# A two-layer hybrid block: the Fourier branch folded about the middle, three kinds of products as plain float32, steps reordered

## The chip, the cores and the metric

The kernel runs on one core of a Trainium2 chip. The metric is device time in microseconds (us) of one execution; lower is better. Engines are named PE or TensorE (matrix products; PEld is its weight load), DVE or VectorE, ACT or ScalarE, POOL or GpSimd, and SP or SyncE, whose queue issues nearly all transfers from HBM.

## The reference, cut to what matters

A backbone block of two layers over 512 latent tokens and 256 context tokens, 1024 channels, all float32. Each layer has a token-mixing part and a SwiGLU part. The mixing part projects the normed and modulated tokens (one matrix, 1792 columns) into three groups:

- A, 512 channels: a depthwise convolution, then an RG-LRU in both directions. Its gates are `sigmoid(xh @ wa + ba)` and `sigmoid(xh @ wx + bx)` with 64 x 64 blocks per head and direction.
- B, 256 channels: spatial gating. In chunks of 128 positions, `s = ws[h] @ v + bs`, with v normed, then `u * s`.
- C, 256 channels in four heads of 64: the Fourier branch, below.

```python
def fourier_mix(xf, wf):
    Bsz, L, _ = xf.shape
    z = xf.reshape(Bsz, L, H_C, HEAD_DIM).astype(jnp.float32)
    f = jnp.fft.fft2(z, axes=(1, 3), norm="ortho").real
    return jnp.einsum("blhc,hce->blhe", f, wf.astype(jnp.float32)).reshape(Bsz, L, D_C).astype(xf.dtype)
```

The three group outputs are RMS-normed, joined and projected by `w_out`. In the second layer the context is only read: its gates and scans are computed, the rest of its mixing is not.

## The kernel before

Tokens lie in six tiles of 128 positions: two of context, four of latents; the second layer's mixing handles the four latent tiles and runs only the RG-LRU over all six. The tokens are kept transposed (`XT`, channel by token), as a high and a low float32r part. `mm` forms a product from three float32r products, high x high, high x low, low x high (`self.pe.matmul`, all recorded on line 134). So every operand needs two parts: `split` copies the rounded value (ScalarE, line 208) and subtracts it from the source (line 203; VectorE or GpSimd, by `wsub` for weights). `split_psum` does the same out of PSUM (lines 873 to 878). A float32 operand can also be given to `matmul` as it is, which the kernel does for the modulation blocks (`mod_part`), the position rows at the start, sums over channels and diagonals.

`mixing` runs one letter of `STEPS[l]` after the other. The letters that matter: `a` the last of four projections with convolution (the first three come from the stage before); `e` the four gates of one 128-channel block of group A (`lru_gates`); `p` the activations of a block's scans, `s` one direction of its scan (`lru_scans`); `Z`, `V`, `U` take weights, `z` projects one half of the Fourier channels, `v` and `u` two tiles of the gating's halves; `f`, `w` small maps of the Fourier and gating branches; `c` the Fourier products over channels; `g` one gate projection of group A's output; `m` one modulation block; `R` rows of the gate after the output projection; `t` the spatial products; `L` releases all gelus, which until then are held so that ScalarE's tables need not change; a digit sets how much of the SBUF arena the loads leave free; `D` moves the weights' subtracts to VectorE.

While `pe.fixed` is true TensorE keeps exactly this written order; each other engine has an in-order queue whose order the framework chose when it built the program. Behind the steps, in the old kernel, come the transposes of group B (`put_group`), the sums of squares of group A, and `fourier`: per tile of positions, products with full cosine and sine matrices (12 products of 256 columns for a context tile, 24 for a latent tile), an RMS norm of that tile (`rms`: ScalarE square, GpSimd power, VectorE scale), transposes and a split. Group A's scaling (`group_a`) stands between the context and the latent tiles. Then `pe.fixed` ends and the output projection follows; its products, as soon as their operands stand, may slip ahead into gaps.

Weights are 512 KB units in a written list (`plan`), loaded ahead on SP's queue as the arena has room, and split when used or up to two units earlier. The output weights (`out`) are scaled and split by ScalarE (line 1353) and VectorE (line 1354). `psum_aux` has two buffers, `psum_big` three.

Of the kernel before, what the change touches and what calls it, by code (L numbers as in the profile page):

```python
# [45 lines left out]
BETWEEN = 2  # L46
# [114 lines left out]
class Kernel:  # L161
# [133 lines left out]
    def consts(self):  # L295
# [21 lines left out]
        self.spl = cp.tile([P, 2, 8], F32, tag="spl", name="spl")  # L317

# [461 lines left out]
    def conv_split(self, cv):  # L780
        xh, xl = self.buf(TOK), self.buf(TOK)
        self.split(xh.r, xl.r, cv[0].f)
        cv += [xh, xl]

    def lru_gates(self, l, m, cv):
        nc, par = self.nc, self.par
        u = self.gw[m // 2]
        if len(cv) == 1:
            self.conv_split(cv)
        xc, xh, xl = cv  # L790
# [14 lines left out]
        xh.free()  # L805
        xl.free()
# [73 lines left out]
    def fourier_maps(self, l):  # L880
# [3 lines left out]
        bd = [self.buf(512), self.buf(512)]  # L884
# [4 lines left out]
        self.split_psum(bd[0].r, bd[1].r, ps)  # L889
# [3 lines left out]
    def gating_maps(self, l):  # L893
        u = self.use(f"sg{l}")
        ws = [self.buf(512), self.buf(512)]
# [3 lines left out]
        self.split_psum(ws[0].r, ws[1].r, ps)  # L899
# [3 lines left out]
    def fourier_in(self, u, lo):  # L903
# [19 lines left out]
    def fourier(self, l, tiles, zc, between):  # L923
# [615 lines left out]
```

## Time and profile before

| | |
|---|---|
| median of 3 runs | 1506.51 us (1502.71 to 1507.05) |
| the profiled execution | 1506.1 us, its span 1504.1 us |
| TensorE busy | 1416.7 us, 94% of the span |
| VectorE busy | 893.4 us |
| ScalarE busy | 551.7 us |
| GpSimd busy | 294.8 us |
| mean granted TensorE clock | 0.974 of 2.4 GHz |
| read from HBM | 160.25 MB |

The span reaches from the first to the last instruction; the execution's own time lies 2.0 us above it. A busy TensorE is not one at its peak: matrix products are pipelined, and their recorded lengths overlap. A granted clock of 1.00 is 2.4 GHz, 0.50 is 1.2 GHz; a mean between them is a mixture of the two over time.

### The profile page before, as it was taken

The numbers are of one execution on the slowest core, as the hardware profiler recorded it, in microseconds if no ns is written. First come the engines' busy times: TensorE is split into PE (matmuls) and PEld (weight loads), VectorE is DVE, ScalarE is ACT, GpSimd is POOL, SyncE is SP. The second block draws the span as 40 slices with busy tenths as digits, with TensorE's granted clock in tenths as the row PEclk, the third lists the DMA queues.
The fourth block names the chain that finished last, engine by engine and source line by source line (L and its number), as shares of the span: only waits on it lengthen the run. The fifth ranks groups of instructions, "written<-read, shape, count | busy, mean of one in ns | idle before, by whom it ended". The sixth has DMA issues, their size and how long they took to land.

```text
span 1504.1 us, 18734 instructions
## 1 busy us (share of the span) xinstructions
PE 1416.7 (94%) x7527; PEld 1197.2 (80%) x7527; DVE 893.4 (59%) x1259; ACT 551.7 (37%) x784; POOL 294.8 (20%) x190
## 2 busy tenths in 40 slices
PE   6999888999999999999999998959998999999997
PEld 3788756779888888888888878858777888888885
DVE  6749756779527439443527396688788343353427
ACT  4576445345312202111203146886536232322210
POOL 3303323230021030030030044223230111020201
PEclk9999999999999999999999999969999999999999
DMA  9503365317116216244127004015427352242201
GB/s 329 139 15 99 105 224 186 97 31 236 43 43 211 70 55 198 71 139 162 36 77 231 28 29 128 1 48 169 127 67 228 98 154 71 70 130 60 77 14 56
DMA packets 169430, 163.56 MB, mean 109 GB/s; under 512 B 10456, under 2 KB 126648, under 8 KB 169344
## 3 DMA queue, kind: packets, MB, share of 16 engines
q1 hardware_dynamic: 169232, 162.08, 34.4%
q8 instruction: 59, 0.97, 0.3%
q0 software_dynamic: 112, 0.30, 0.1%
q14 instruction: 27, 0.22, 0.0%
HBM read 160.25 MB, written 2.10 MB: 108 GB/s over the span
## 4 chain that ended last, share of the span: by engine, by line
PE 72%; DVE 12%; ACT 5%; issue 3%; DMA 3%; POOL 3%; SPq 2%; DVEq 0%; POOLq 0%; ACTq 0%
PE mm L134 67%; PE aux L134 5%; POOL smalls L232 2%; DVE f L678 1%; DVE f L203 1%; DVE f L1220 1%; DMA f<-in_w_in_dram 1%; DVE r L203 1%; SPq L1315 1%; POOL r L203 1%; SPq L1333 1%; DVE f L832 1%; DVE smalls L709 1%; ACT r L208 1%; DVE f L835 1%
## 5 line engine op out<-in xcount | busy, mean ns | idle before, releaser
L134 PE MATMUL mm<-r,r 128*128 128x512 f32 (+1 forms) x6192 | 1230.6, 360 | 21.0 <-DVE f L1220 7.3
L134 PEld LDWEIGHTS mm<-r,r 128*128 128x128 f32 x6192 | 1035.7, 191 | 202.0 <-DVE f L1220 12.5
L208 ACT ACTIVATE r<-f 128x1024 fp32r<-128x1024 f32 (+2 forms) x244 | 227.1, 951 | 578.0 <-PE mm L134 267.9
L203 DVE TENSOR_TENSOR r<-f,r 128x1024 fp32r<-128x1024 f32 (+3 forms) x245 | 266.8, 1111 | 133.8 <-ACT r L208 119.9
L203 POOL TENSOR_TENSOR f<-f,f 128x1024 f32<-128x1024 f32 (+2 forms) x44 | 109.7, 2493 | 654.3 <-DVE f L1220 479.3
L1220 DVE TENSOR_TENSOR f<-mm,f 128x512 f32<-128x512 f32 (+1 forms) x80 | 76.2, 952 | 145.2 <-PE mm L134 145.1
L203 POOL TENSOR_TENSOR r<-f,r 128x1024 fp32r<-128x1024 f32 (+2 forms) x59 | 107.0, 1823 | 226.0 <-ACT r L208 159.3
L1235 DVE TENSOR_TENSOR f<-mm,f 128x768 f32<-128x768 f32 (+1 forms) x44 | 36.2, 823 | 176.0 <-PE mm L134 176.0
L134 PE MATMUL aux<-r,r 128*128 128x256 f32 (+1 forms) x780 | 112.5, 306 | 25.3 <-DVE r L878 10.7
L134 PEld LDWEIGHTS aux<-r,r 128*128 128x128 f32 x780 | 106.5, 211 | 32.5 <-DVE r L878 12.7
L232 POOL TENSOR_TENSOR smalls<-smalls,neghalf 128x1 f32<-128x1 f32 (+2 forms) x69 | 67.2, 975 | 255.1 <-DVE smalls L231 245.7
L573 DVE SCALAR_TENSOR_TENSOR f<-f,stc,f 128x512 f32<-128x512 f32 x140 | 102.3, 762 | 2.8 <-DMA f<-in_w_mod_dram 1.3
L203 DVE TENSOR_TENSOR f<-f,f 128x512 f32<-128x512 f32 (+1 forms) x66 | 61.7, 939 | 9.8 <-ACT f L801 8.1
L1234 ACT ACTIVATE f<-mm 128x768 f32<-128x768 f32 (+1 forms) x44 | 30.7, 699 | 95.7 <-PE mm L134 95.7
L134 PE MATMUL aux<-cst,f 128*128 128x128 f32 (+2 forms) x259 | 38.7, 282 | 25.1 <-ACT f L644 8.7
L659 ACT ACTIVATE f<-aux,modT 128x128 f32<-128x128 f32 x128 | 48.5, 466 | 33.3 <-PE aux L134 33.3
L134 PEld LDWEIGHTS aux<-cst,f 128*128 128x128 f32 (+2 forms) x259 | 29.7, 143 | 37.3 <-ACT f L644 11.5
L644 ACT ACTIVATE f<-f,smalls 128x1024 f32<-128x1024 f32 x19 | 23.6, 1242 | 90.8 <-DVE smalls L643 90.8
L777 DVE SCALAR_TENSOR_TENSOR f<-mm,par,f 128x255 f32<-128x255 f32 (+3 forms) x48 | 26.1, 605 | 17.4 <-ACT f L771 17.4
L623 DVE BATCH_NORM_STATS2 smalls<-f 128x6 f32<-128x512 f32 x44 | 28.4, 682 | 5.0 <-DMA f<-in_ctx_dram 4.6
L801 ACT ACTIVATE f<-mm,par 128x768 f32<-128x768 f32 x32 | 28.0, 903 | 6.5 <-PE mm L134 5.0
L832 DVE SCALAR_TENSOR_TENSOR f<-f,f 128x768 f32<-128x768 f32 x16 | 22.2, 1390 | 12.7 <-ACT f L831 12.7
(117 smaller groups left out, 628.3 us busy)
## 6 DMA issues: line engine op xcount, KB each, us to landing
f<-in_w_mod_dram SPq DMA_DIRECT2D x96, 512.0 KB
f<-in_w_up_dram SPq DMA_DIRECT2D x88, 512.0 KB
f<-in_w_down_dram SPq DMA_DIRECT2D x40, 512.0 KB
f<-in_w_in_dram SPq DMA_DIRECT2D x28, 512.0 KB
f<-in_w_out_dram SPq DMA_DIRECT2D x16, 512.0 KB
f<-in_b_mod_dram SPq DMA_DIRECT2D x6, 512.0 KB
f<-in_x_dram SPq DMA_DIRECT2D x4, 512.0 KB
f<-in_k_cosl_dram SPq DMA_DIRECT2D x4, 512.0 KB
```

The lines of the kernel that those rows point to most:

```text
L134: i = f(*args, **kw)
L203: return eng.tensor_tensor(out=out, in0=a, in1=b, op=op)
L208: i = self.nc.scalar.activation(h, src, AF.Copy)
L232: self.nc.gpsimd.tensor_tensor(out=out, in0=v, in1=self.neghalf[:, 0:n], op=ALU.pow)
L573: nc.vector.scalar_tensor_tensor(out=b.f, in0=w, scalar=c, in1=b.f, op0=ALU.mult, op1=ALU.add)
L623: nc.vector.bn_stats(out=st[:, c, :], in_=x[:, c * 512 : (c + 1) * 512])
L659: nc.scalar.activation(y.f[:, q * P : (q + 1) * P], ps[:, q * P : (q + 1) * P], AF.Identity, bias=self.modT[:, slot, k, s : s + 1], scale= ...
L801: insts.append(nc.scalar.activation(g.f, ps[:, 256:1024], AF.Sigmoid, bias=par[:, col : col + 1]))
L832: nc.vector.scalar_tensor_tensor(out=t_.f, in0=r.f, scalar=1.0, in1=t_.f, op0=ALU.add, op1=ALU.mult)
L1220: self.nc.vector.tensor_tensor(out=tb.f, in0=ps[:, c], in1=m[:, c], op=ALU.mult)
L1234: nc.scalar.activation(g.f, pg[:, 256 + lo : 1024], AF.Silu)
L1235: nc.vector.tensor_tensor(out=g.f, in0=pu[:, 256 + lo : 1024], in1=g.f, op=ALU.mult)
```

## The change

The gates (32 products of 768 columns), the Fourier branch and the spatial products no longer use high and low parts: each is one plain float32 product, and the splits of their operands go.

The Fourier branch uses that a cosine is even and a sine odd about the middle of a sequence. `fourier_in` adds to each position its mirror image for the cosine half and subtracts it for the sine half, so that the channel products (`fourier_cols`) run over half of the tiles each (one folded tile for the context, two for the latents), and the position products (`fourier_positions`) make only the first half of the output positions, channel by position, for 130 or 258 columns; the other half is cosine part minus sine part, written backwards. The position in the middle is handled by itself (`fourier_middle`). The output comes out transposed, so its transposes go; its RMS norm is done like group A's, with sums of squares over channels by products with ones (`rms_rows`) and a product with a diagonal (`rms_put`), for all tiles at once. One constant (`k_dft`, 860 KB, of which the second layer loads 727 KB) takes the place of five and four loads of 512 KB.

The steps are put in another order, with new letters: `F` positions of one segment, `A` and `N` sums of group A and of the Fourier group, `B`, `Q`, `P` their scalings and group B's transposes, `O` the weights' subtracts back to GpSimd, `H` and `h` the weights' high copies to GpSimd and back to ScalarE. Two of three sums of squares of group A in each layer move from GpSimd to VectorE, the diagonals from VectorE to GpSimd. In the second layer all gate projections now stand ahead of `L`.

```diff
-STEPS = ("feaekZeeppzssz6ssgpgpsssVvvsvUuuumgmcLccw7RmtgmmmD", "faeekeeZpsspszzcsppVcssvvgULusDsugwgtg")
+STEPS = ("feaeZeeppzssz8shgpmOsgs6p7sVsshvUv6HuvDcLmu8F6gHDc8cFwhuNRmtgDmAQmBmP", "ZaHfeepzszVpssvcecegwsvppUDsFuhugsgDsgs6L7NAtQBP")
...
+        elif eng == "pool":
+            i = self.nc.gpsimd.tensor_scalar(out=h, in0=src, scalar1=1.0, scalar2=0.0, op0=ALU.mult, op1=ALU.add)
...
-    def conv_split(self, cv):
-        xh, xl = self.buf(TOK), self.buf(TOK)
-        self.split(xh.r, xl.r, cv[0].f)
-        cv += [xh, xl]
...
-                lh = (u.high.r[:, c : c + P], u.low.r[:, c : c + P])
-                self.mm(ps[:, 256:512], lh, (xh.r[:, 0:256], xl.r[:, 0:256]), True, True)
-                self.mm(ps[:, 512:1024], lh, (xh.r[:, 256:768], xl.r[:, 256:768]), True, True)
+                for lo, hi in ((0, 256), (256, 768)):
+                    self.pe.matmul(ps[:, 256 + lo : 256 + hi], u.low.f[:, c : c + P], xc.f[:, lo:hi], start=True, stop=True)
...
-        zt = (self.buf(TOK), self.buf(TOK))
-        self.split_psum(zt[0].r[:, lo:], zt[1].r[:, lo:], pz[:, 256 + lo : 1024])
-        return zt
+        z = self.buf(TOK)
+        self.nc.scalar.activation(z.f[:, lo:], pz[:, 256 + lo : 1024], AF.Copy)
+        for s, n in self.segments(tiles):
+            h = n // 2
+            mirror = pz[:, 256 + s + n - 1 : 256 + s + h : -1]
+            self.nc.vector.tensor_tensor(out=z.f[:, s + h + 1 : s + n], in0=z.f[:, s + 1 : s + h], in1=mirror, op=ALU.subtract)
+            self.nc.vector.tensor_tensor(out=z.f[:, s + 1 : s + h], in0=z.f[:, s + 1 : s + h], in1=mirror, op=ALU.add)
+        return [z]
+
+    def fourier_middle(self, tiles, bd, zt):
+
+        ps = self.psum_aux()
+        at = slice(128, 513, 384) if tiles[0] == 0 else slice(512, 514)
+        for k in range(2):
+            self.pe.matmul(ps[:, 2 * k : 2 * k + 2], bd[0].f[:, k * 256 : k * 256 + P], zt[k][0].f[:, at], start=True, stop=True)
+        self.nc.vector.tensor_copy(self.middle, ps[:, 0:4])
+        return 1 if tiles[0] == 0 else 0
+
+    def fourier_cols(self, at, bd, zt):
+
+        zc = [self.buf(512)]
+        ps = self.psum_aux()
+        for c in range(2):
+            for k in range(2):
+                o = ps[:, c * 256 + k * P : c * 256 + (k + 1) * P]
+                self.pe.matmul(o, zt[k][0].f[:, at[c] : at[c] + P], bd[0].f[:, k * 256 + c * P : k * 256 + (c + 1) * P], start=True, stop=True)
+        self.nc.scalar.activation(zc[0].f, ps, AF.Copy)
+        return zc
+
+    def fourier_positions(self, i, n, u, zc, y, sq):
...
+        for k in range(2):
+            ps = self.psum_big()
+            for c in range(2):
+                for j in range(nj):
+                    mat = slice(o + (c * nj + j) * w, o + (c * nj + j + 1) * w)
+                    e = slice(c * 256 + k * P, c * 256 + (k + 1) * P)
+                    self.pe.matmul(ps[:, c * 512 : c * 512 + w], zc[j][0].f[:, e], u.low.f[:, mat], start=j == 0, stop=j == nj - 1)
...
+            nc.vector.scalar_tensor_tensor(out=t.f, in0=sign, scalar=self.middle[:, m : m + 1], in1=ps[:, 0:w], op0=ALU.mult, op1=ALU.add)
+            nc.vector.tensor_tensor(out=y[k].f[:, s : s + h + 1], in0=t.f[:, 0 : h + 1], in1=ps[:, 512 : 512 + h + 1], op=ALU.add)
+            nc.vector.tensor_tensor(out=y[k].f[:, s + n - 1 : s + h : -1], in0=t.f[:, 1:h], in1=ps[:, 513 : 512 + h], op=ALU.subtract)
+            t.free()
+            nc.scalar.activation(sq[k].f[:, s : s + n], y[k].f[:, s : s + n], AF.Square)
...
+    def rms_rows(self, tiles, sq, width):
...
+            for i, b in enumerate(sq):
+                self.pe.matmul(ssum[:, n : n + 1], b.f[:, ti * P : (ti + 1) * P], self.ones[:, 0:1], start=i == 0, stop=i == len(sq) - 1)
...
+            nc.gpsimd.tensor_scalar(out=dg.f[:, n * P : (n + 1) * P], in0=self.ident, scalar1=r[:, n : n + 1], scalar2=None, op0=ALU.mult)
...
-        nc.vector.tensor_tensor(out=zv, in0=zv, in1=wide(rs), op=ALU.mult)
-        H, L = (b.r.rearrange("p (h n c) -> p h n c", h=4, c=64)[here] for b in vb)
-        self.split(H, L, src)
+        by = rs.rearrange("p (n h) -> p h n", n=2).unsqueeze(3).to_broadcast([P, 4, 2, 64])
+        nc.vector.tensor_tensor(out=j, in0=src, in1=by, op=ALU.mult)
...
-            self.mm(o, lh, tuple(b.r[:, h * n_t * 64 : (h + 1) * n_t * 64] for b in vb), True, True)
+            self.pe.matmul(o, ws[0].f[:, h * P : (h + 1) * P], vb[0].f[:, h * n_t * 64 : (h + 1) * n_t * 64], start=True, stop=True)
...
-                    self.tt(nc.gpsimd if m < MA - 1 else nc.vector, sq[0].f[:, lo:], sq[0].f[:, lo:], g.f[:, lo:], ALU.add)
+                    self.tt(nc.vector, sq[0].f[:, lo:], sq[0].f[:, lo:], g.f[:, lo:], ALU.add)
...
+            us.append(Unit(f"dft{l}", DFT_COLS, load, raw=True))
```

## Rows read from the trace of the kernel before

**Rows 1.** The page's first part: busy time of each engine, share of the span, instructions.

```profile
PE 1416.7 (94%) x7527; PEld 1197.2 (80%) x7527; DVE 893.4 (59%) x1259; ACT 551.7 (37%) x784; POOL 294.8 (20%) x190
```

**Rows 2.** Stretches: PE, PEld, DVE, ACT, POOL busy; granted clock, DMA share, GB/s.

```profile
72.00:212.00 140.00, 126.19 (x767) 106.51 (x767) 95.75 (x109) 83.06 (x105) 29.52 (x12) 0.93 0.29 91
212.00:269.00 57.00, 48.54 (x321) 37.79 (x318) 36.18 (x79) 30.30 (x66) 21.46 (x21) 0.97 0.65 220
949.00:1080.00 131.00, 107.93 (x616) 94.98 (x616) 100.45 (x137) 100.19 (x138) 32.80 (x21) 0.88 0.27 85
400.00:860.00 460.00, 460.00 (x2470) 398.71 (x2469) 224.47 (x285) 91.49 (x102) 62.20 (x25) 1.00 0.35 109
```

**Rows 3.** TensorE in order of time, layer 0: start, length, line, work, count, wait.

```profile
168.71 13.84 PE L134 MATMUL aux<-r,r 128*128 128x256 f32 x96 [4.73 <-ACT f L981]
...
238.80 1.50 PE L134 MATMUL aux<-ones,f 128*128 128x1 f32 x12
...
245.81 1.50 PE L134 MATMUL mm<-f,ones 128*128 128x128 f32 x12
247.07 3.12 PE L134 MATMUL aux<-r,r 128*128 128x256 f32 x24
...
251.56 3.05 PE L134 MATMUL aux<-r,r 128*128 128x256 f32 x24
254.45 0.62 PE L134 MATMUL mm<-r,r 128*128 128x512 f32 x2
...
264.07 3.22 PE L134 MATMUL mm<-r,r 128*128 128x512 f32 x12
```

**Rows 4.** TensorE in order of time, layer 1, same columns.

```profile
940.06 10.68 PE L134 MATMUL mm<-r,r 128*128 128x256 f32 x60
...
984.65 0.80 PE L134 MATMUL aux<-r,r 128*128 128x256 f32 x2 [6.76 <-ACT r L877]
...
1000.69 14.21 PE L134 MATMUL aux<-r,r 128*128 128x256 f32 x96 [6.10 <-DVE r L878]
1014.74 5.63 PE L134 MATMUL mm<-r,r 128*128 128x512 f32 x24
1020.21 11.68 PE L134 MATMUL aux<-r,r 128*128 128x256 f32 x96
...
1053.37 0.82 PE L134 MATMUL aux<-cst,f 128*128 128x128 f32 x6
...
1075.02 4.00 PE L134 MATMUL mm<-r,r 128*128 128x512 f32 x15
...
1079.57 23.76 PE L134 MATMUL mm<-r,r 128*128 128x512 f32 x103
```

**Rows 5.** The chain that ended last, two pieces: start, length, what.

```profile
224.30 5.91 DMA f<-in_k_cosl_dram
...
951.94 15.08 PE mm L134 x84
```

**Rows 6.** TensorE in order of time, the start of the program.

```profile
6.80 7.17 PE L134 MATMUL mm<-f 8*128 8x512 f32 x8
13.91 3.67 PE L134 MATMUL mm<-cst,f 128*128 128x128 f32 x16
```

**Rows 7.** VectorE's groups by form, 949 to 1080 us: busy, mean ns, idle before.

```profile
L832 DVE SCALAR_TENSOR_TENSOR f<-f,f 128x768 f32<-128x768 f32 x8 | 12.5, 1558 | 7.3 <-ACT f L831 7.3
...
L1354 DVE SCALAR_TENSOR_TENSOR r<-f,par,r 128x1024 fp32r<-128x1024 f32 x6 | 7.7, 1278 | 0.0
...
L1080 DVE TENSOR_TENSOR f<-f,f 128x512 f32<-128x512 f32 x4 | 2.7, 683 | 0.1
```

**Rows 8.** GpSimd and VectorE in order of time around 154 us.

```profile
153.53 5.94 POOL L203 TENSOR_TENSOR r<-f,r 128x1024 fp32r<-128x1024 f32 x2 [12.40 <-issue]
...
154.25 2.98 DVE L203 TENSOR_TENSOR f<-f,f 128x768 f32<-128x768 f32 x1
...
160.21 0.95 DVE L834 SCALAR_TENSOR_TENSOR f<-f,f 128x768 f32<-128x768 f32 x1
```

More of the change, by code (lines that the diff above doesn't have):

```diff
@@ L317, in consts @@
         self.spl = cp.tile([P, 2, 8], F32, tag="spl", name="spl")
+        self.middle = cp.tile([P, 4], F32, tag="middle", name="middle")
     def XT(self, a, b):
@@ new lines, in rms_rows @@
+    def rms_rows(self, tiles, sq, width):
+        nc = self.nc
+        n_t = len(tiles)
+        ssum = self.psum_aux()
+        for n, ti in enumerate(tiles):
+            for i, b in enumerate(sq):
+                self.pe.matmul(ssum[:, n : n + 1], b.f[:, ti * P : (ti + 1) * P], self.ones[:, 0:1], start=i == 0, stop=i == len(sq) - 1)
+        for b in sq:
+            b.free()
+        r = self.small(n_t)
+        self.rstd(r, ssum[:, 0:n_t], 1.0 / width, EPS)
+        dg = self.buf(n_t * P)
+        for n in range(n_t):
+            nc.gpsimd.tensor_scalar(out=dg.f[:, n * P : (n + 1) * P], in0=self.ident, scalar1=r[:, n : n + 1], scalar2=None, op0=ALU.mult)
+        return dg
@@ new lines, in rms_put @@
+    def rms_put(self, tiles, dg, ys, k0):
+        nc = self.nc
+        lo = tiles[0] * P
+        pr = self.psum_big()
+        for n, ti in enumerate(tiles):
+            self.pe.matmul(pr[:, 256 + ti * P : 256 + (ti + 1) * P], self.ones, dg.f[:, n * P : (n + 1) * P], start=True, stop=True)
+        dg.free()
+        for m, y in enumerate(ys):
+            nc.vector.tensor_tensor(out=y.f[:, lo:], in0=pr[:, 256 + lo : 1024], in1=y.f[:, lo:], op=ALU.mult)
+            for a, b in ((0, NC_T), (NC_T, NT)):
+                if a >= tiles[0]:
+                    H, L = (x[:, :, k0 + m, :] for x in self.XT(a, b))
+                    src = y.f[:, a * P : b * P].rearrange("p (t n) -> p t n", n=P)
+                    nc.scalar.activation(H, src, AF.Copy)
+                    self.tt(nc.gpsimd if k0 + m in (0, 2) else nc.vector, L, src, H.bitcast(F32), ALU.subtract)
+            y.free()
@@ L1047, in mixing @@
             cv.append(self.conv(m, ps))
-            self.conv_split(cv[m])
         hs = {}
@@ L1063, in mixing @@
         zt, zc, uv, ws = [], [], {"v": [], "u": []}, []
+        segs, yf, qf, fu = self.segments(tiles), [], [], []
+        folded = [(s + j * P, s + n // 2 + j * P) for s, n in segs for j in range(n // 2 // P)]
+        self.middle_at = None
+        diag, gated = {}, []
         m2b, rows = gate_rows or ([], [])
@@ L1092, in step @@
             elif x == "z":
-                zt.append(self.fourier_in(held["z"].pop(0), lo))
+                zt.append(self.fourier_in(held["z"].pop(0), tiles))
             elif x == "s":
@@ L1134, in step @@
             elif x == "t":
+                assert not self.late and len(uv["u"]) == len(uv["v"]) == n_t // 2 and ws
                 self.gating(tiles, uv["u"], vb, ws)
+                gated.append(1)
             elif x == "L":
@@ L1370, in dft, with load @@
         def dft(l):
-            for nm in ("k_cosl", "k_sinl"):
-                for q in range(2):
-                    us.append(Unit(f"{nm}{l}.{q}", 1024, dma(t[nm][:, q * 1024 : (q + 1) * 1024], "p n -> p n")))
+            a = DFT_CTX if l == DEPTH - 1 else 0
+            def load(b):
+                nc.sync.dma_start(out=b[:, a:], in_=t["k_dft"][:, a:])
+            us.append(Unit(f"dft{l}", DFT_COLS, load, raw=True))
         def params(l):
@@ L1422, in plan @@
                     spatial(l)
+                elif x == "F" and us[-1].name != f"dft{l}" and f"dft{l}" not in [u.name for u in us]:
+                    dft(l)
                 elif x in "UV":
```

180 lines of the change are left out of this document (70 added, 110 removed).

## The prediction

> **What bounds the kernel now.** I read the page's table of engines first: TensorE is busy for 1416.7 of 1504.1 us [rows 1]. Its 87 us of idle time are not spread evenly, so the second view is the busy time by stretch [rows 2]. The SwiGLU parts leave nothing: from 400 to 860 us TensorE is busy throughout, at the full 2.4 GHz, and the change does not touch that code. Both mixing parts lie otherwise. Layer 0, from 72 us (convolutions) to 269 (the first uninterrupted output projection), has 13.8 us idle up to the gating step at 212 and 8.5 behind it, at mean granted clocks of 0.93 and 0.97: some 0.14 x 140 + 0.06 x 57 = 23 us passed at 1.2 GHz. Layer 1 (949 to 1080) has 23.1 us idle and a clock of 0.88, or 31 us at 1.2 GHz. Work at half clock loses half its time: up to 11.5 and 16 us, less where the slow time was idle anyway. Idle and slow clock together are at most 73 us; that and TensorE's own work is all the change can touch.
>
> Third, TensorE in order of time shows what the idle time waits for. In layer 1 the Fourier column products stand still 6.8 us for a ScalarE copy and 6.1 us for a VectorE subtract: both make high and low parts, both queued behind the RG-LRU's activations and scans [rows 4]. In layer 0 a 4.7 us wait is for the copy that frees a small PSUM buffer [rows 3]. The chain also has 5.9 us for a load of a Fourier matrix [rows 5]. VectorE is the second engine: 100 of 131 us in layer 1 [rows 2].
>
> **TensorE, term by term.** Of float32r products, 84, half of 256 and half of 512 columns, take 15.08 us in the chain [rows 5], so six (one gate of 768 columns in three products each) take 1.08 us; 24 of 256 columns take 2.89 us to the start of the next work, 0.12 each. A plain float32 product stands in the trace as two instructions: twelve of 128 columns start at 245.81 and the next work at 247.07 [rows 3]: 0.105 each, 0.21 us per 128 columns.
> - Gates, 32 of them: 32 x 6 x 0.21 = 40.3 for 34.5 us: +5.8.
> - Fourier positions: 216 x 0.12 = 25.9 us go. The folded ones stream 4 x 130 + 2 x 8 x 258 = 4648 columns: 7.6 us. -18.3.
> - Fourier columns: 60 x 0.12 = 7.2 go; five tiles of four 128-column products, 4.2, and some 1.0 for the middle: -2.0.
> - Normalisation of the branch: two sums per tile where none was, 40 instructions at 0.125 (twelve in 1.50 us [rows 3]), and ten diagonals of two at 0.105: +7.1. Its 20 transposes go, at 0.14 (six in 0.82 us [rows 4]): -2.8.
> - Spatial products: one product of four times the column price for three: within 1 us, taken as 0.
>
> Sum: -10 us. The unseen form is plain float32 of 512 columns over 128 rows. Below: 0.42 us per instruction (the 128-column row times four). Above: the 8-row position products of the start, 7.17 / 8 = 0.90 [rows 6]. There sixteen transposes take 3.67 us, 0.23 each for 0.14 later, so that row was read at a slower clock, and I take the lower.
>
> **VectorE and ScalarE.** The change removes eight 768-column splits, ten splits of Fourier columns, four of the branch, four of gate weights, four of maps and five of normed gating values, each a ScalarE copy and a subtract, mostly on VectorE, of 0.68 us per 512 columns to 0.95 per 768 [rows 7, 8]. It adds on VectorE twelve mirrored adds and subtracts and six combinations for each of three segments (up to 258 columns, so under 0.5 each), scaling and split of the Fourier output by whole rows, and four square sums from GpSimd. For layer 1: out 3 x 0.95 within the stretch, 7 x 0.68 for columns, maps and normed values, and 3.7 of per-tile Fourier work; in 4 + 6 pieces at 0.45, 4 x 0.68, 2 x 0.68: about -3 of 100 us, so it relieves little by volume. It does take both engines out of the way between two TensorE steps: the Fourier columns need one copy behind them, not copy and subtract.
>
> **Order and queues.** The plain matrices are one 860 KB load (727 KB in layer 1) in place of five and four of 512 KB, asked for on SP's queue where the first folded product stands in the steps, ahead of the part's last weights. The 5.9 us wait goes; if the load is late, the positions wait, and with them everything behind in TensorE's fixed order. Fourier columns and positions move up between projections, and so does their cover: the positions (23 us in layer 0, 11.5 in layer 1, at 0.12) that stood under the group normalisation and the preparation of output weights are gone from the end.
>
> Layer 1: the part's first work starts 0.8 ahead of 940.06. Up to the step that releases the held gelus TensorE has 0.8 (maps), 8.5 (convolution projection: 48 of the 60 there), 20.2 (gates), 11 (two projections at 5.47), 23.4 (four gating inputs at 5.84), 21.9 (four gates at 5.47), 2.2, 3.4 and 0.5 (columns, positions, spatial maps) = 92 us [rows 4]. With 5 us of gaps it is there at 1036. Nothing large is left for it behind (about 7 us), while VectorE, at 0.68 per 512 columns, has two gating norms of four (5.4), four gate products and three sums (4.8), the gating with its norms, as 7 (4.7), Fourier output (2.7), group A (4.1), group B (1.4) = 23 us, and part of eight output-weight splits at 1.28 [rows 7]. I take 26: output projection at 1062 for 1079.6. But 17 of its products, the last 15 in 4.00 us, had already slipped into gaps [rows 4]: -13.6, so -14.
>
> Layer 0: up to 212, TensorE's 126.2 busy us hold up to 9.8 of slow clock; 116 + 2.9 (gates) - 1.3 (columns) + 4.2 (positions, from behind) + 3 (their sums) = 125; half the 23.6 of gaps and slow clock stay: 137 for 140, -3. Behind it (57 us) TensorE has only a gate projection, three modulation blocks and small work, some 21 us, and VectorE 34 of its 36.2. With 37.5 us that is -19.5, less 23 output products at 0.235 (5.4), twelve of them at 264.07 [rows 3]: -14. Splits ahead of the stage: -1.
>
> Sum: -14 - 3 - 14 - 1 = -32. The profiled execution lasted 1506.1 us, 2.0 around its span; the median is 1506.5: **1474 us**. It goes from 1463 (layer 1 without new gaps, its end 6 shorter) to 1486 (gaps of 10, end 5 longer, layer 0 end 2.5 longer).
>
> **A rule against it.** At 154.25 a VectorE operation on two tiles of 768 columns takes 2.98 us, against 0.95 for one at 160.21; GpSimd runs two weight subtracts from 153.53 to 159.47 [rows 8]. In layer 1 one group's mean is 1.56 [rows 7]. The Trainium skill (SBUF — State Buffer, Who interferes with whom) says that a VectorE operation with two SBUF inputs and a GpSimd one that reads SBUF exclude each other for a whole instruction. By that rule, which these rows agree with, the copies newly put on GpSimd stretch VectorE too.
>
> **The rivals.**
> - *Better: only the bare ends stay idle.* Both stages hold, at full clock, (174.7 - 11.5) + (107.9 - 15.7) = 255 us of TensorE; -10, plus 18 and 12 us bare at the ends = 275 for 328: -53, **1453**. For it: most of the long waits are for the removed splits. Against: the modulation blocks' own chain and the RG-LRU queues stay.
> - *Bare tail.* In layer 1 the gelus wait for the last square root, then norm after norm; TensorE falls to 1.2 GHz meanwhile. The end takes 40 instead of 26 us, layer 0's 8 more: **1496**.
> - *The other side: GpSimd blocks VectorE.* New there: the high copies of about 10 weights and 20 diagonals. Each can cost a VectorE operation 2.0 us as at 154.25. All 30 on VectorE's path: +60, **1534**; it decides from 16 on, which eats the 32. Against: four square sums leave GpSimd, and it is busy for 51 of 197 and 33 of 131 us only [rows 2].
> - *Plain products at the upper bound* [rows 6]: the gates cost 40 us more: **1514**.
>
> **How the numbers follow.** Chances: forecast 0.52, better 0.22, bare tail 0.17, GpSimd 0.05, dear products 0.04. 0.3% (4.5 us) is what a measurement here can tell from no change. Faster: 0.52 + 0.22 + 0.13 of the tail = 0.87; same 0.03 and slower 0.10, from the tail's rest, GpSimd and the products. The range, 1446 to 1498, holds forecast, better case and most of the tail; outside are the last two rivals and fringes, under 0.2.
>
> **What the profile would show.** Right: plain 512-column products 0.43 us apart; no 6 us wait at the Fourier columns; positions under 10 us; just ahead of each output projection a gap of 10 to 20 us with VectorE full, and a lower clock there. Wrong: idle time within the stages as large as before (45 us), VectorE's 768-column means above 1.6, a wait for the Fourier matrix, or SwiGLU stretches that change by more than a few us.

## The result and the profile after

The changed kernel takes 1484.04 us (median of 4 runs) against 1504.61 for the kernel before: a ratio of 0.9865, 95% interval [0.9838, 0.9891], or 20.6 us less. The forecast was 1474, its likeliest case 1463 to 1486. The profiled executions have spans of 1481.4 and 1504.1 us, 22.7 apart.

The page's table of engines, to be read beside [rows 1]:

```profile
PE 1403.3 (95%) x7307; PEld 1172.6 (79%) x7307; DVE 865.3 (58%) x1230; ACT 517.4 (35%) x719; POOL 288.2 (19%) x199
```

Busy time by stretch, with the columns of [rows 2]; the stretches are the same parts of the program, moved to where they now lie, and layer 1's is cut in two at its last gate projection:

```profile
72.00:212.00 140.00, 130.02 (x769) 107.69 (x771) 88.04 (x114) 79.59 (x98) 27.64 (x17) 0.94 0.29 92
212.00:254.00 42.00, 38.26 (x216) 26.18 (x208) 29.05 (x57) 23.34 (x43) 14.53 (x18) 0.91 0.72 236
400.00:860.00 460.00, 459.91 (x2446) 396.67 (x2445) 235.93 (x305) 90.88 (x103) 62.30 (x28) 1.00 0.34 107
936.00:1023.00 87.00, 83.19 (x436) 67.37 (x435) 65.33 (x78) 68.22 (x84) 16.07 (x9) 0.98 0.14 45
1023.00:1049.00 26.00, 11.32 (x58) 8.79 (x56) 18.97 (x40) 13.17 (x25) 16.77 (x16) 0.73 0.34 102
```

TensorE's idle time in the two mixing parts is 10.0 + 3.7 + 3.8 + 14.7 = 32 us where it was 45 [rows 2]. In layer 1 it has changed its place: up to the last gate projection TensorE works almost without a gap, and then stands bare for 14.7 of 26 us, at a mean clock of 0.73, until the output projection.

TensorE in order of time, layer 0 (start, length, line, work, count, wait):

```profile
84.06 15.64 PE L137 MATMUL mm<-f,f 128*128 128x256 f32 x48
99.13 17.48 PE L137 MATMUL mm<-r,r 128*128 128x256 f32 x98
...
163.54 7.50 PE L137 MATMUL aux<-r,r 128*128 128x256 f32 x48 [3.64 <-ACT f L1010]
...
181.06 1.06 PE L137 MATMUL mm<-f,f 128*128 128x130 f32 x8
...
193.71 3.32 PE L137 MATMUL mm<-f,f 128*128 128x258 f32 x14 [0.97 <-ACT f L937]
...
213.09 1.74 PE L137 MATMUL aux<-f,f 128*128 128x384 f32 x4
...
230.04 2.69 PE L137 MATMUL aux<-ones,f 128*128 128x1 f32 x12 [2.66 <-DVE f L206]
...
254.30 8.06 PE L137 MATMUL mm<-r,r 128*128 128x512 f32 x34 [0.35 <-DVE r L1385]
```

The same view from the hand-over at the end of layer 0's SwiGLU part to the end of layer 1's output projection:

```profile
897.06 1.09 PE L137 MATMUL aux<-cst,f 128*128 128x128 f32 x8 [2.24 <-ACT f L650]
...
908.56 1.89 PE L137 MATMUL aux<-cst,f 128*128 128x128 f32 x8 [3.65 <-ACT f L650]
...
934.34 2.75 PE L137 MATMUL mm<-f,f 128*128 128x256 f32 x8
...
963.19 1.16 PE L137 MATMUL aux<-f,f 128*128 128x128 f32 x8 [0.78 <-ACT f L1010]
...
977.11 2.93 PE L137 MATMUL mm<-f,f 128*128 128x256 f32 x4 [2.71 <-ACT f L799]
...
991.75 3.65 PE L137 MATMUL mm<-f,f 128*128 128x258 f32 x16
...
1006.76 16.51 PE L137 MATMUL mm<-r,r 128*128 128x512 f32 x72
...
1035.91 1.84 PE L137 MATMUL aux<-ones,f 128*128 128x1 f32 x8 [10.96 <-DVE f L206]
...
1049.00 30.39 PE L137 MATMUL mm<-r,r 128*128 128x512 f32 x123 [1.42 <-ACT r L996]
...
1112.16 1.09 PE L137 MATMUL aux<-cst,f 128*128 128x128 f32 x8 [3.42 <-ACT f L650]
```

Two of the long waits of [rows 4] were at the Fourier columns, 6.76 and 6.10; at 963.19 one of 0.78 is left. No wait for the Fourier matrix is seen, where [rows 5] had 5.91. What stands now is the bare end, a wait of 2.71 for a gate's sigmoid, and at the hand-over waits of 2.24 and 3.65 for a norm. The last of these is not new: in the kernel before, TensorE has these rows at the same two norms:

```profile
912.04 1.09 PE L134 MATMUL aux<-cst,f 128*128 128x128 f32 x8 [0.85 <-ACT f L644]
...
921.66 1.97 PE L134 MATMUL aux<-cst,f 128*128 128x128 f32 x8 [3.37 <-ACT f L644]
```

GpSimd in order of time, at the hand-over and in layer 1:

```profile
888.85 6.18 POOL L206 TENSOR_TENSOR r<-f,r 128x1024 fp32r<-128x1024 f32 x3
894.99 0.54 POOL L237 TENSOR_TENSOR smalls<-smalls,neghalf 128x1 f32<-128x1 f32 x1
...
898.03 2.94 POOL L206 TENSOR_TENSOR r<-f,r 128x1024 fp32r<-128x1024 f32 x1 [0.63 <-ACT r L211]
...
904.88 2.34 POOL L206 TENSOR_TENSOR r<-f,r 128x1024 fp32r<-128x1024 f32 x1
...
970.35 1.89 POOL L213 TENSOR_SCALAR r<-f 128x1024 fp32r<-128x1024 f32 x1 [38.58 <-ACT f L799]
972.32 2.92 POOL L206 TENSOR_TENSOR r<-f,r 128x1024 fp32r<-128x1024 f32 x1
```

and VectorE beside these, and later at the bare end:

```profile
898.66 3.40 DVE L684 SCALAR_TENSOR_TENSOR f<-f,smalls,f 128x1024 f32<-128x1024 f32 x1
...
904.94 2.29 DVE L649 SCALAR_TENSOR_TENSOR smalls<-smalls 128x1 f32<-128x1 f32 x1 [0.66 <-POOL smalls L237]
...
971.36 4.70 DVE L206 TENSOR_TENSOR f<-f,f 128x768 f32<-128x768 f32 x2
...
1029.49 0.69 DVE L1044 TENSOR_TENSOR f<-f,smalls 128x512 f32<-128x512 f32 x1 [1.54 <-POOL smalls L237]
```

VectorE's groups by form, 925 to 1053 us, the one of [rows 7] with two inputs of 768 columns:

```profile
L828 DVE SCALAR_TENSOR_TENSOR f<-f,f 128x768 f32<-128x768 f32 x8 | 8.6, 1070 | 4.8 <-ACT f L827 4.8
```

Its mean is 1.07 us for 1.56 before. At the hand-over a norm's power (894.99), which takes half a microsecond, stood behind three weight subtracts. Two more subtracts lie beside two VectorE operations of the last norm's chain, 898.66 and 904.94; what these take without a subtract beside them, run e9 shows below. In layer 1 the new copy on GpSimd and the subtract behind it lie beside two VectorE operations that take 4.70 us together, where such an operation elsewhere takes 0.95 [rows 8]; the sigmoid wait of 2.71 follows them.

To see where time goes in all runs, I cut each trace at four events on ScalarE: the first gate sigmoid and the first SiLU of each layer. The table has the five stretches in us: the start, mixing of layer 0 with its output projection, SwiGLU of layer 0 with the hand-over, mixing of layer 1, SwiGLU of layer 1. The ratio is that of times, to the kernel before.

| kernel | start | mix 0 | SwiGLU 0 | mix 1 | SwiGLU 1 | ratio |
|---|---|---|---|---|---|---|
| before | 73.5 | 289.9 | 587.6 | 195.0 | 358.1 | 1 |
| after | 72.0 | 271.0 | 593.4 | 186.2 | 358.8 | 0.9865 |
| e1 gates alone | 71.9 | 294.8 | 590.1 | 209.8 | 358.5 | 1.0125 |
| e6 the same, other reserve | 71.4 | 288.7 | 592.3 | 212.3 | 356.8 | 1.0099 |
| e12 fold alone | 76.5 | 281.7 | 586.0 | 209.6 | 356.1 | 1.0044 |
| e2 both, old order | 73.3 | 285.4 | 599.3 | 205.4 | 357.1 | 1.0114 |
| e3 gates back, new order | 73.8 | 283.6 | 592.5 | 194.3 | 359.6 | 1.0027 |
| e7 old order in layer 1 | 72.4 | 271.0 | 586.2 | 203.1 | 359.4 | 0.9916 |
| e8 old order in layer 0 | 73.5 | 285.6 | 594.7 | 193.1 | 357.3 | 1.0007 |
| e5 before, other reserve | 79.0 | 299.3 | 591.8 | 209.5 | 357.7 | 1.0184 |
| e11 after, other reserve | 71.8 | 279.8 | 596.2 | 184.3 | 358.2 | 0.9927 |
| e4 after, no H in layer 1 | 71.8 | 270.9 | 593.3 | 182.7 | 358.8 | 0.9827 |
| e9 e4, Z later | 73.3 | 269.9 | 586.6 | 189.2 | 359.4 | 0.9846 |
| e10 e4, scans earlier | 71.4 | 270.4 | 593.0 | 194.0 | 355.9 | 0.9892 |

So by these spans the change took 1.4 us at the start, 18.9 in layer 0 and 8.8 in layer 1, and gave 5.8 back in the SwiGLU stretch of layer 0, whose own products it does not touch.

### The profile page after: what moved, and what is told of

Same layout as the page of the kernel before. It is cut to its first block, busy times and chain, and to the rows that moved or that the text cites. A ratio compares the mean times of both kernels' runs of the same rounds, so it can differ in the third digit from the quotient of the medians.

```text
span 1481.4 us, 18151 instructions
## 1 busy us (share of the span) xinstructions
PE 1403.3 (95%) x7307; PEld 1172.6 (79%) x7307; DVE 865.3 (58%) x1230; ACT 517.4 (35%) x719; POOL 288.2 (19%) x199
## 4 chain that ended last, share of the span: by engine, by line
PE 76%; DVE 12%; ACT 5%; issue 4%; POOL 3%; DMA 1%; SPq 0%; DVEq 0%; ACTq 0%; POOLq 0%
PE mm L137 71%; PE aux L137 5%; POOL smalls L237 2%; DVE f L206 1%; DVE f L684 1%; POOL r L206 1%; DVE r L206 1%; DVE f L1251 1%; DVE f L831 1%; DVE smalls L715 1%; ACT f L665 1%; DVE f L828 1%; DVE r L1385 1%; DVE f L830 1%; ACT f L818 1%
## 5 line engine op out<-in xcount | busy, mean ns | idle before, releaser
L137 PE MATMUL mm<-r,r 128*128 128x512 f32 (+1 forms) x6000 | 1198.0, 361 | 20.2 <-DVE f L1251 6.5
L211 ACT ACTIVATE r<-f 128x1024 fp32r<-128x1024 f32 (+2 forms) x210 | 195.0, 953 | 560.2 <-PE mm L137 197.2
L206 DVE TENSOR_TENSOR r<-f,r 128x1024 fp32r<-128x1024 f32 (+2 forms) x232 | 252.1, 1109 | 148.4 <-ACT r L211 123.7
L206 POOL TENSOR_TENSOR f<-f,f 128x1024 f32<-128x1024 f32 x40 | 99.6, 2490 | 636.4 <-DVE f L1251 606.2
L206 POOL TENSOR_TENSOR r<-f,r 128x512 fp32r<-128x512 f32 (+2 forms) x52 | 90.0, 1738 | 136.9 <-DVE f L828 45.9
L237 POOL TENSOR_TENSOR smalls<-smalls,neghalf 128x1 f32<-128x1 f32 (+3 forms) x61 | 61.9, 1016 | 246.0 <-DVE smalls L236 245.6
L137 PE MATMUL aux<-r,r 128*128 128x256 f32 x480 | 60.7, 288 | 3.6 <-ACT f L1010 3.6
L137 PEld LDWEIGHTS aux<-r,r 128*128 128x128 f32 x480 | 59.7, 196 | 4.9 <-ACT f L1010 3.8
L137 PE MATMUL aux<-cst,f 128*128 128x128 f32 (+1 forms) x239 | 35.3, 284 | 22.7 <-ACT f L650 12.0
L137 PE MATMUL mm<-f,f 128*128 128x512 f32 (+3 forms) x168 | 52.8, 467 | 4.0 <-ACT f L799 3.0
L137 PEld LDWEIGHTS aux<-cst,f 128*128 128x128 f32 (+1 forms) x239 | 28.1, 144 | 31.4 <-ACT f L650 14.6
L783 DVE SCALAR_TENSOR_TENSOR f<-mm,par,f 128x255 f32<-128x255 f32 (+3 forms) x48 | 25.7, 611 | 21.8 <-ACT f L777 21.8
```

What stands on the lines that cost most here:

```text
L137: i = f(*args, **kw)
L206: return eng.tensor_tensor(out=out, in0=a, in1=b, op=op)
L237: self.nc.gpsimd.tensor_tensor(out=out, in0=v, in1=self.neghalf[:, 0:n], op=ALU.pow)
L783: nc.vector.scalar_tensor_tensor(out=o, in0=ps[:, i0 : i0 + o1 - o0], scalar=w(k), in1=o, op0=ALU.mult, op1=ALU.add)
```

## The experiments

**Products and order apart.** Four runs undo the change by parts. Plain gates alone, in the kernel before:

```diff
...
-        xc, xh, xl = cv
+        xc = cv[0]
...
-                self.mm(ps[:, 256:512], lh, (xh.r[:, 0:256], xl.r[:, 0:256]), True, True)
-                self.mm(ps[:, 512:1024], lh, (xh.r[:, 256:768], xl.r[:, 256:768]), True, True)
+                for lo, hi in ((0, 256), (256, 768)):
+                    self.pe.matmul(ps[:, 256 + lo : 256 + hi], u.low.f[:, c : c + P], xc.f[:, lo:hi], start=True, stop=True)
...
-MIX_RESERVE = (12000, 9000)
+MIX_RESERVE = (14000, 9000)
...
```

> The kernel before with one part of the change alone: the gates as plain float32, with their splits gone; high and low parts everywhere else, the old order, and 2000 more columns kept free in the first mixing part. Theory: 32 gates at 1.26 us in place of 1.08 cost TensorE 5.8 us, and the eight splits that go give back about as much in the waits of layer 1, so the ratio to the kernel before is 0.997 to 1.002. Rival, the gates carry the gain because their splits held ScalarE and VectorE: 0.993 or less. Rival, plain products are dear: 1.005 or more.

Measured: 1.0125 [1.0103, 1.0148], 19 us slower. My theory missed. The rival's number holds, but not its reason: the gates are no dearer than forecast (in the changed kernel, above, 48 instructions from 84.06 to 99.13, 5.02 us for each group of four gates; in this run the same 48 take 15.07 us too), and mixing of layer 1 became 14.8 us longer for 2.9 us of added products.

All products changed, the steps in the old order:

```diff
-STEPS = ("feaeZeeppzssz8shgpmOsgs6p7sVsshvUv6HuvDcLmu8F6gHDc8cFwhuNRmtgDmAQmBmP", "ZaHfeepzszVpssvcecegwsvppUDsFuhugsgDsgs6L7NAtQBP")
+STEPS = ("feaeZeeppzssz6ssgpgpsssVvvsvUuuumgmcLccw7RmtgmmmDPAFBFNQ", "faeeeeZpsspszzcsppVcssvvgULusDsugwgtgPAFBNQ")
...
-        self.reserve = 7000
+        self.reserve = 8000
```

> The changed kernel with the steps of the kernel before: every product as after the change, the fold included, but the Fourier columns, positions and norms where they stood (positions and group A's scaling at the end), and the weights' copies on ScalarE; 1000 more columns kept free behind the steps. Theory: TensorE's 10 us less and the shorter chain between two TensorE steps give about half of the gain, the order the other half: ratio to the kernel before 0.990 to 0.996. Rival, the products alone do it: 0.985 to 0.988. Rival, the order alone does it: 0.998 or more.

Measured: 1.0114 [1.0098, 1.0131]. A miss again: with every product of the change but not its order, the kernel is 17 us slower than before. The second rival's number holds; the next run speaks against its reason.

The changed kernel with the gates as high and low parts again (the gate weights are split again with them):

```diff
         xc = cv[0]
+        xh, xl = self.buf(TOK), self.buf(TOK)
+        self.split(xh.r, xl.r, xc.f)
...
-                for lo, hi in ((0, 256), (256, 768)):
-                    self.pe.matmul(ps[:, 256 + lo : 256 + hi], u.low.f[:, c : c + P], xc.f[:, lo:hi], start=True, stop=True)
+                lh = (u.high.r[:, c : c + P], u.low.r[:, c : c + P])
+                self.mm(ps[:, 256:512], lh, (xh.r[:, 0:256], xl.r[:, 0:256]), True, True)
+                self.mm(ps[:, 512:1024], lh, (xh.r[:, 256:768], xl.r[:, 256:768]), True, True)
...
```

> The changed kernel with the gates back in high and low parts, each block's values split where its gates are computed, in the new order. Theory: TensorE has 5.8 us less to do, ScalarE and VectorE 0.83 and 0.95 us more per block, ahead of the gates; in layer 1, where VectorE sets the end, that costs about 4 us, in layer 0 TensorE wins 2 to 3: ratio to the kernel before 0.985 to 0.989, about as after the change. Rival, TensorE's work counts one to one: 0.983 or less. Rival, the splits count in full: 0.990 or more.

Measured: 1.0027 [1.0015, 1.0038]; the second rival holds. In the new order the plain gates, which cost TensorE 6 us, are worth 24. TensorE in order of time shows how, in each layer:

```profile
169.41 13.45 PE L137 MATMUL aux<-r,r 128*128 128x256 f32 x96 [16.55 <-ACT f L1015]
...
984.38 6.55 PE L137 MATMUL mm<-r,r 128*128 128x256 f32 x23 [7.17 <-DVE r L206]
...
1056.94 1.84 PE L137 MATMUL aux<-ones,f 128*128 128x1 f32 x8 [14.15 <-DVE f L206]
```

and VectorE just ahead of the second wait's end:

```profile
982.13 1.28 DVE L841 TENSOR_TENSOR_SCAN f<-f,f,f 128x512 f32<-128x512 f32 x1
983.32 0.14 DVE L931 COPY middle<-aux 128x4 f32<-128x4 f32 x1
983.37 0.95 DVE L206 TENSOR_TENSOR r<-f,r 128x768 fp32r<-128x768 f32 x1
```

The subtract that makes the gate's low part takes 0.95 us; it stands behind the scans, and TensorE waits 7.17 for it. In layer 0 the wait of 16.55, where the changed kernel has 3.64, is for a gelu's read on ScalarE (168.76), which itself began straight behind two such subtracts on VectorE (1.80 us from 166.87).

The fourth corner is the fold without the plain gates, in the old order (the edits of the last two runs together, with the reserve of 7000 left):

> The folded Fourier branch and the plain spatial products in the old order of steps, with the gates as high and low parts (the letters A, B, N, Q, P and F of the new code put at the ends of the old order). With the kernel before, plain gates alone, all products without the new order, and the changed kernel with its gates back, this is the fourth corner. Theory (what counts is whether the steps are set for the products, and no part carries a gain of its own): ratio to before 0.997 to 1.010. Rival (the fold is the gain, by its shorter positions and its missing splits, and only the plain gates hurt in the old order): 0.983 to 0.992.

Measured: 1.0044 [1.0027, 1.0061], as the theory said. In the old order the plain gates, the fold and both together are all slower than the kernel before; in the new order both together gain 0.0135 and the fold without them loses 0.0027. As measured, no part has a price that could be added to another's. These corners also differ in how much memory they keep back, which is looked at below.

**The order, layer by layer.** Old steps in layer 1 alone, and in layer 0 alone:

```diff
# e7: the second string of STEPS
-"ZaHfeepzszVpssvcecegwsvppUDsFuhugsgDsgs6L7NAtQBP"
+"faeeeeZpsspszzcsppVcssvvgULusDsugwgtgPAFBNQ"
# e8: the first string of STEPS, and the reserve behind it
-"feaeZeeppzssz8shgpmOsgs6p7sVsshvUv6HuvDcLmu8F6gHDc8cFwhuNRmtgDmAQmBmP"
+"feaeZeeppzssz6ssgpgpsssVvvsvUuuumgmcLccw7RmtgmmmDPAFBFNQ"
-        self.reserve = 7000
+        self.reserve = 8000 if l == 0 else 7000
```

> The changed kernel with the old order of steps in layer 1 alone (its new letters A, B, N, Q, P and F put at the end). With the old order in both layers the stretches from layer 1's first sigmoid to its first Silu were 205.4 us against 186.2. Theory (each layer's order acts in its own stage): that stretch becomes 203 to 208 us and the total 1501 to 1506, ratio to before 0.997 to 1.001. Rival (the loss of the old order sits where layer 0 hands over): total within 5 us of the changed kernel, ratio 0.986 to 0.990.

> The changed kernel with the old order of steps in layer 0 alone (and 8000 columns kept back behind it in place of 7000, which the memory asks for). With the old order in both layers, layer 0's mixing was 14.5 us longer than in the changed kernel, and the SwiGLU stretch behind it 5.8. Theory (each layer's order acts in its own stage): those two again, total 1501 to 1507, ratio 0.997 to 1.002. Rival (layer 1 carries it all): total below 1492, ratio under 0.991.

Measured: 0.9916 [0.9903, 0.9930] and 1.0007 [0.9996, 1.0019]. Layer 0's order is worth 21 us by its ratio and layer 1's 7.7; both together, in e2, some 37. In e7 layer 1's mixing has the length that the theory said, but the total lies between the two expectations, since the SwiGLU stretch of layer 0 is 7.2 us shorter. The total of e8 lies in the theory's range, and that is partly luck: layer 0's mixing is 14.6 us longer, as said, but the SwiGLU stretch only 1.3 and not 5.8, and layer 1's mixing, whose steps e8 does not touch, is 6.9 longer. So not each order acts in its own stage alone; why layer 1 loses in e8 is not shown. TensorE in order of time in e7:

```profile
902.48 1.09 PE L137 MATMUL aux<-cst,f 128*128 128x128 f32 x8 [0.40 <-ACT f L650]
...
968.61 0.59 PE L137 MATMUL aux<-f,f 128*128 128x2 f32 x2 [8.81 <-DVE f L916]
```

At the hand-over the last norm is waited for 0.40 us, not 3.65: what is given back there goes, with layer 0 in the new order, with the new order of layer 1. And the wait ahead of the Fourier columns is back, 8.81 us, now for the fold's first mirrored operation on VectorE (0.41 us), which stands behind the scans as the low-part subtract did. e2 has it too, with 8.82, and e12 with 9.01. So it is not the folded product that did away with the 6 us waits of [rows 4], but where it stands among the scans.

In e8 the stretch from the gating step to the output projection is the poor one (columns as in [rows 2]):

```profile
215.00:270.00 55.00, 40.43 (x198) 31.21 (x191) 31.94 (x52) 21.71 (x33) 16.39 (x19) 0.78 0.28 91
```

with waits of 4.71 us for a square on ScalarE and 3.37 for a diagonal on GpSimd.

**When weights are prepared.** A number of the kernel before that changes no arithmetic, only how much memory layer 0's mixing keeps back before the next weight is asked for:

```diff
-MIX_RESERVE = (12000, 9000)
+MIX_RESERVE = (16000, 9000)
```

> The kernel before with one number changed: the free columns that layer 0's mixing keeps back before it asks for the next weight, 16000 in place of 12000. Nothing is computed in another way. It asks whether the 19 us that the plain gates alone lost came from the gates or from when weights are loaded and prepared (that run kept back 14000). Theory (the planner's loads only shift work that is hidden): ratio to before 0.997 to 1.003. Rival (a shift of the loads by itself moves the stages by tens of us): outside 0.993 to 1.007.

Measured: 1.0184 [1.0163, 1.0204], 28 us slower: the rival. All stretches up to layer 1's SwiGLU part are longer. TensorE in order of time at the start and behind layer 1's output projection:

```profile
64.75 12.30 PE L134 MATMUL mm<-r,r 128*128 128x256 f32 x53 [2.24 <-POOL r L203]
...
1168.02 1.97 PE L134 MATMUL aux<-cst,f 128*128 128x128 f32 x8 [4.86 <-ACT f L644]
```

The first is a weight whose low part is late, the second a norm; these two are examples, and most of the 28 us is not accounted for here. So e1's loss could have been its reserve, and I ran it again:

```diff
-MIX_RESERVE = (14000, 9000)
+MIX_RESERVE = (13000, 9000)
```

> Plain gates alone in the kernel before, as in the run that lost 19 us, but with 13000 columns kept back in layer 0's mixing in place of 14000. Theory (the gates in the old order cost the time, whatever the reserve): ratio to before 1.010 to 1.015 again. Rival (that run's loss was its reserve): 0.995 to 1.003.

Measured: 1.0099 [1.0085, 1.0113], at the theory's lower edge. The loss of the plain gates in the old order stands at two reserves, both above the 12000 of the kernel before, at which it was not measured. The same 16000 in the changed kernel:

> The changed kernel with 16000 in place of 12000 columns kept back at the start of layer 0's mixing, the same edit that cost the kernel before 28 us. Theory (both kernels hang on when weights are prepared, and the steps were set for one such order): 5 to 30 us slower than the changed kernel, ratio to before 0.990 to 1.006. Rival (the changed kernel, with fewer split weights, is less bound to it): within 4 us of it, ratio 0.984 to 0.989.

Measured: 0.9927 [0.9914, 0.9941], 9 us slower than the changed kernel: the theory, at a third of the size that the kernel before showed.

**Versions that might be better.** Weights' high copies on ScalarE in layer 1, as before the change:

```diff
-"ZaHfeepzszVpssvcecegwsvppUDsFuhugsgDsgs6L7NAtQBP"
+"ZafeepzszVpssvcecegwsvppUDsFuhugsgDsgs6L7NAtQBP"
```

> The changed kernel with one letter taken out: in layer 1 the weights' high copies stay on ScalarE instead of GpSimd. Theory: in the changed kernel a copy and three subtracts in a row on GpSimd (887.7 to 895.0 us) stand in front of the power that the last norms ahead of layer 1 wait for, and three TensorE waits there (0.95, 2.24, 3.65 us) are longer for it than before; without the copies 1 to 4 us come back, ratio to the kernel before 0.984 to 0.986. Rival, these copies are off the path: 0.987 as after the change; or ScalarE takes their place as the late engine: 0.988 or more.

Measured: 0.9827 [0.9811, 0.9844]; 1479.49 us, 4.5 less than the changed kernel and the best here. The theory looked for the gain at the hand-over, and it is not there: that stretch takes 593.3 us as before, and the last two norms are waited for 3.13 and 5.22. Of the 3.9 us between the spans 3.5 are in layer 1's mixing. VectorE and GpSimd at the place of the pairs shown above:

```profile
970.89 1.81 DVE L206 TENSOR_TENSOR f<-f,f 128x768 f32<-128x768 f32 x2
```

```profile
970.89 4.03 POOL L206 TENSOR_TENSOR r<-f,r 128x1024 fp32r<-128x1024 f32 x1 [39.63 <-ACT r L211]
...
977.33 2.40 POOL L206 TENSOR_TENSOR r<-f,r 128x1024 fp32r<-128x1024 f32 x1 [2.41 <-ACT r L211]
```

The two VectorE operations take 1.81 us in place of 4.70; GpSimd's subtract beside them takes 4.03 where the next takes 2.40. One of the two engines pays. The 2.71 us wait for the sigmoid is gone, and the output projection starts at 1044.97.

On top of it, the Fourier branch's weights are asked for later in layer 1:

```diff
-"ZafeepzszVpssv..."
+"afeeZpzszVpssv..."
```

> The changed kernel without the letter H of layer 1 (the weights' copies stay on ScalarE there, as in the run that gained 4.5 us) and with layer 1 beginning a, f, e, e, Z, p in place of Z, a, f, e, e, p: the two weights of the Fourier branch, which are split, are no longer the first to be prepared while the SwiGLU part of layer 0 ends; the gates' weights, which are not split, come first. Theory (the 6 us given back at that hand-over are GpSimd's subtracts of these two weights among the norms' powers, since they were not there with layer 1's old order): the stretch from layer 0's first Silu to layer 1's first sigmoid becomes 586 to 589 us from 593.3, the total 1473 to 1476, ratio to before 0.979 to 0.981. Rival (the weights are only prepared later, and layer 1's start waits for them): the stretch shorter, layer 1's mixing longer by as much, ratio 0.982 to 0.984.

Measured: 0.9846 [0.9830, 0.9862], no better than e4. The hand-over did what the theory said (586.6 us), and the output projection starts 3.7 us earlier; but layer 1's mixing ends where it did. VectorE ahead of the last norm of the hand-over, to be read beside 898.66 and 904.94 of the changed kernel:

```profile
896.56 1.28 DVE L684 SCALAR_TENSOR_TENSOR f<-f,smalls,f 128x1024 f32<-128x1024 f32 x1
...
900.79 0.16 DVE L649 SCALAR_TENSOR_TENSOR smalls<-smalls 128x1 f32<-128x1 f32 x1 [0.73 <-POOL smalls L237]
```

TensorE in order of time:

```profile
895.48 1.09 PE L137 MATMUL aux<-cst,f 128*128 128x128 f32 x8 [1.82 <-ACT f L650]
...
902.40 1.09 PE L137 MATMUL aux<-cst,f 128*128 128x128 f32 x8
...
1041.26 34.82 PE L137 MATMUL mm<-r,r 128*128 128x512 f32 x140 [2.24 <-ACT r L996]
...
1108.67 1.97 PE L137 MATMUL aux<-cst,f 128*128 128x128 f32 x8 [6.84 <-ACT f L650]
```

The last norm ahead of the SwiGLU part is waited for 6.84 us, where e4 has 3.40. VectorE is busy for 18.68 of the 20 us from 1088 to 1108 (15.88 in e4), and the last tile's statistics start at 1103.41, in e4 at 1103.20: other work of VectorE that e4 does later now stands ahead of them. So the mixing became 6.5 us longer, about what the hand-over gave, as the rival said, but not because its start waits.

Scans one place earlier, on top of e4:

```diff
-"...gwsvppUDsFuhugsgDsgs6L7NAtQBP"
+"...gwspvpUDssFuhugsgDs6gL7NAtQBP"
```

> The changed kernel without the letter H of layer 1 and with the third scan group's start and two scan steps one place earlier in layer 1, so that the held gelus are released straight behind the last gate's projection with no scan between. Theory (layer 1's bare end is VectorE's queue from the last scans on: work moved ahead of it shortens the end): output projection 4 to 6 us earlier against the run that only leaves H out (1044.97), total 1472 to 1476, ratio 0.978 to 0.981. Rival (VectorE is full from 998 us on, so the scans only push the gating norms back): within 2 us of that run, ratio 0.982 to 0.984.

Measured: 0.9892 [0.9876, 0.9908]. Neither theory's number. The bare end grew, by this row of TensorE:

```profile
1033.91 1.84 PE L137 MATMUL aux<-ones,f 128*128 128x1 f32 x8 [15.09 <-DVE f L206]
```

against 11.47 in e4, and the uninterrupted output projection starts at 1051.11. Ahead of it VectorE waits 3.89 us for the power of the last gating norm: GpSimd makes four diagonals first (3.42 us from 1024.98). In e4 that power comes ahead of the diagonals, and VectorE waits 1.54. The rest of the loss was not followed.

## Why the prediction was right, and where its steps were not

The time lies in the stated range, 10 us above the forecast; the gain is two thirds of what was forecast, 20.6 of 32 us.

**TensorE's terms.** The plain gate has its forecast price: 5.02 / 4 = 1.26 us. The folded positions take 1.06 + 4.0 + 3.65 = 8.7 us for a forecast 7.6. The sum of -10 cannot be tested by the busy time: it fell by 13.4 us, but e2, with the same products, is busy for 1415.6 us (see the last section).

**Layer 1: place and tail right, size not.** The gates begin at 934.34 and the last gate projection ends at 1023.3, 88.9 us later for a forecast 87.4; from there to the output projection it is 25.7 us, forecast 26. VectorE is not full in that tail: 19 of 26 us; of the rest 3.1 are waits for GpSimd's powers (1.54 each at two norms), and most of what is left are short waits for TensorE. The stage still gained 8.8 and not 14: the first 123 products of the output projection take 30.39 us, 0.247 each, at a mean granted clock of 0.95 behind the bare end, where 103 took 23.76, 0.231 each [rows 4], at 1.00; and the norm ahead of the SwiGLU part is waited for 3.42 us.

**Layer 0: sum right, its parts not.** Forecast -18 with the start, measured -20.3. From the first sigmoid to the gating step it is 2.4 us longer than before, not 3 shorter; behind it 41.2 us for 56.4, with 13 products more slipped in, together some 18 us for a forecast 14 (an estimate, at 0.235 a product as in the prediction). That these errors nearly cancel is luck. The gap of 10 to 20 us that was expected ahead of each output projection came in layer 1 alone: in layer 0 TensorE is idle there for 3.7 of 42 us.

**The term that was missing.** The sum had nothing for the hand-over at the end of layer 0's SwiGLU part, which gave back 5.8 us; a SwiGLU stretch that changes by more than a few us was among the signs of being wrong. TensorE is idle for 2.8 us more in it (9.4 for 6.6) and busy for 3.1 us more, with 14 more products recorded. The new order asks for the Fourier branch's two split weights first. e9, which against e4 moves these alone, takes 6.7 us off the stretch, and e7, with all of layer 1's old order, 7.2; but with layer 0 in its old order too it does not hold, for e2 has 599.3 us where e8 has 594.7. What the weights' subtracts do in the changed kernel is of two kinds: three stand ahead of a norm's power on GpSimd (894.99), and two lie beside operations of the last norm on VectorE, which take 3.40 and 2.29 us where in e9 they take 1.28 and 0.16. These 4.25 us lie in front of the wait of 3.65, which is gone in e9. The kernel before has one such pair there: VectorE's one-column operation takes 2.29 us from 918.04, beside a subtract from 917.97. The hand-over and layer 1's 5.2 make up the difference: 32 - 5.8 - 5.2 - 0.7 (SwiGLU of layer 1) + 2.3 (layer 0) = 22.6, the 22.7 of the spans.

**The reason that was wrong.** I wrote that the change "take[s] both engines out of the way between two TensorE steps" at the Fourier columns. In the old order it does not: the waits there are 8.81 (e7), 8.82 (e2) and 9.01 us (e12). The new order does away with them, and by e3's 7.17 us wait only with the plain gates. The forecast walked through the new order stage by stage; a sum over the parts of the diff would have had no footing in these runs.

**The rivals.** "Only the bare ends" failed at the layer-0 gaps, the lower clock and the hand-over. The bare tail did not come in layer 1 (25.7, not 40). "GpSimd blocks VectorE" is real at single places and the forecast had no term for it: the copies of layer 1 cost 3.5 us in its mixing by e4, and the last norm of the hand-over 4.25 us on VectorE. It is far from the 16 conflicts from which it decides, and it is not new on the whole: VectorE operations that overlap GpSimd work and take over 0.3 us more than the shortest of their form lose 52.6 us in the kernel before and 47.5 in the changed one, added up over the traces. How much of that TensorE waited for is not shown. The Trainium skill's rule (SBUF — State Buffer, Who interferes with whom) agrees with those rows: of a two-input VectorE operation and a GpSimd one beside it, one is stretched, 4.70 for 1.81 us on VectorE (a pair), or 4.03 for 2.40 on GpSimd. The same section says that the order of issue decides which of the two blocks; that fits the changed kernel, where GpSimd's copy was 1 us ahead (970.35 against 971.36) and VectorE paid, and is not decided by e4, where both began at 970.89. At the hand-over GpSimd costs by its own queue as well (894.99). Plain products are not dear: 1.26 us a gate. Their upper bound was put too low: 32 gates at 0.90 us per 512 columns in place of 0.42 come to 46 us, not 40.

**What stays open.** e5 shows that the kernel before lies 28 us below itself with another reserve. e1, e2, e6 and e8 keep back more memory at some point than the kernels that they are compared with. How much of what e1, e2 and e12 lose is the products' own order on VectorE (the 9 us wait of e2 and e12 is) and how much is when weights come free and are prepared cannot be told apart by these runs. Nor was the new order tried without the fold, since its steps presuppose the folded products.

## What to carry to other kernels

Where an order is written by hand, price a change by walking through each stage of the new order, the hand-overs included; a part of it undone or done alone tells what it is worth in that order, not what it is worth. Before a per cent is put down to an edit, change a number that computes nothing, and see how far the kernel moves by itself. A gain ahead of a stage whose second engine is full is not a gain at the end: look for the same work landing in front of the next wait. Work moved to GpSimd is paid for in GpSimd's own queue and, where a VectorE operation runs beside it, there too (3.40 us for 1.28 here).

## What was not expected of the hardware

The busy time of the same products is not fixed: the changed kernel and e2 issue 7307 each, and are busy for 1403.3 and 1415.6 us, at mean granted clocks of 0.975 and 0.967. By these means they spent 74 and 100 us at 1.2 GHz, and by the traces TensorE was busy for 55 and 70 us of them; half of the difference, some 7 of the 12 us, is then the clock (an estimate), and the rest is not explained. In layer 1's mixing each kernel's longest time at 1.2 GHz begins in its longest wait: at 1028.2 in the changed kernel, in the 10.96 us, and at 992.0 in e2, in the 8.82 us. There TensorE pays twice, in the wait and in the products behind it.

And how long a tiny operation can take: VectorE's step on one column, 0.16 us in e9, took 2.29 us beside a GpSimd subtract, in the chain of a norm that TensorE waited for.
